# Block-diagonal carried states: one 128-row state product for both heads of a pair

## The chip, the cores and the metric

The kernel runs on one NeuronCore of a Trainium2 chip. The metric is device time in microseconds from start to end of the program; the median of several executions counts. The engines are PE (TensorE, with its weight loads, PEld), DVE (VectorE), ACT (ScalarE), POOL (GpSimd) and SP (SyncE, which issues most DMAs).

## What is computed

Two layers of a hybrid block over 2048 latent and 256 context tokens, 1024 wide. Each layer projects the normed tokens, runs four mixers with four heads of 64 beside each other (differential attention, HGRN2, windowed attention, mLSTM), gates their outputs and projects them back. The change lies in the outputs of two of them. Cut to that, with q, k, v per head and chunk:

```python
# HGRN2: o_t = S_t^T q_t in chunks, forward and backward, then summed
o = (jnp.einsum('bhnls,bhnsv->bhnlv', a, v)                       # within the chunk
     + jnp.einsum('bhnlk,bhnkv->bhnlv', q * jnp.exp(cum), s_start))  # carried state
y = from_heads(rmsnorm(o_f + flip_time(o_b), g))

# mLSTM: each direction has its own denominator
num = (jnp.einsum('bhnls,bhnsv->bhnlv', s, v)
       + g0[..., None] * jnp.einsum('bhnlk,bhnkv->bhnlv', q, c0))  # carried state c0
den = jnp.sum(s, axis=-1) + g0 * jnp.einsum('bhnlk,bhnk->bhnl', q, n0)
hid = num / jnp.maximum(jnp.abs(den), jnp.exp(-m_t))[..., None]
y = rmsnorm(h_f + flip_time(h_b), g) * sigmoid(og)
```

## The kernel before

Tokens are cut into 18 tiles of 128 (16 latent, 2 of context; the second layer needs outputs for 16). Four heads are two pairs (`pr`), and the two heads of a pair (`pa_`) lie in partitions 0 to 63 and 64 to 127 of one tile.

A layer has three stages: the first projections; differential attention, with the other projections as filler between its products; and the final stage. While the last projections run, window attention (`swa_stream`) and mLSTM (`mlstm_stream`) may already do two tiles (`room`, L1227). When the projections are done (`done["rest"]`), their buffers are freed and the output product (`out_stream`) and HGRN (`hgrn_stream`) join. `weave` picks the next step of these streams: each `yield` names a position in tiles, a distance in modelled PE time and a condition, and `mm` (L92) adds to that modelled time by the count of moving columns (four times that for fp32). The order in which each engine gets its instructions comes from a scheduler that works from this written order; each engine then works in order.

`yt_of` hands out one tile of mixed output per token tile, `YTB` of them in all; a stream may begin tile i only while i is less than the number of tiles put out plus `YTB`. HGRN works on groups of two tiles and asks for both.

The carried states at the start of each tile were stored by the projection stage in device memory (`dmC` for mLSTM, 64 x 65 per head, its last column the normalizer; `dhS` for HGRN, 64 x 64). `states_of` (L1232) loads them for two tiles and both directions: one DMA for the forward direction, two for the backward one, whose order is reversed, and a memset where a tile has none before it. The loaded tile has 128 partitions: the two heads of a pair above each other.

In `mlstm_stream`, `mqk` holds the products of keys and queries, DVE multiplies them by the decays in `r1b`, and then for each half `pa_` a PSUM bank `num` takes, for two directions and two pairs, one product of 128 rows (`r1b` by `v1`) and one of the 64 rows of that head (`g0b` by `cst`). ACT takes the absolute denominators, DVE their maximum, reciprocal and the quotient `hd`, and POOL adds the two directions into `yt`. In `hgrn_stream`, for each half a bank `pos` (`go` in the trace) takes for two tiles and two pairs the product within the tile (`Am` by `vi`, 128 rows) and the two directions' state products (`qe` by `hst`, 64 rows), and ACT copies the bank to `O`.

Of the kernel before, what the change touches and what calls it, by code (L numbers as in the profile page):

```python
# [19 lines left out]
YTB, GPB, FXB, EB = 6, 4, 1, 3  # L20
# [13 lines left out]
P = 128  # L34
# [39 lines left out]
def kernel(  # L74
# [29 lines left out]
    def act(o, i, f, **kw):  # L104
        A.activation(out=o, in_=i, func=f, **kw)  # L105
# [153 lines left out]
    for l in range(n_layers):  # L259
# [941 lines left out]
        with ExitStack() as st4:  # L1201
# [30 lines left out]
            def states_of(src, g, n, pool, tag):  # L1232

                st_ = pool.tile([P, 2, 2, 2, n], F32, tag=tag, name=tag, bufs=2)
                for d in range(2):
                    js = [jpos(d, order[2 * g + i]) - 1 for i in range(2)]
                    for i, j in enumerate(js):
                        if j < 0:
                            G.memset(st_[:, d, :, i], 0.0)
                    if min(js) >= 0 and js[0] < js[1]:  # L1240
                        SP.dma_start(st_[:, d], src[d][:, :, js[0]:js[1] + 1])
                    else:
                        for i, j in enumerate(js):
                            if j >= 0:
                                SP.dma_start(st_[:, d, :, i], src[d][:, :, j])
                return st_
# [142 lines left out]
            def mlstm_stream():  # L1389
                nxt = mlstm_load(0)  # L1390
                for i in range(len(order)):
# [3 lines left out]
                    if i % 2 == 0:  # L1395
                        cst = states_of(dmC, i // 2, 65, ml, "cst")
# [10 lines left out]
                    for pa_ in range(2):  # L1407
                        r_ = slice(pa_ * 64, pa_ * 64 + 64)
                        num = bank([P, 4, 65], "mnum")
                        dn = ml.tile([P, 4], F32, tag="dn", name="dn", bufs=4)  # L1410
                        for d in range(2):
                            for pr in range(2):
                                h = pr * 2 + pa_
                                mm(num[:, d * 2 + pr], r1b[:, d, h], v1[:, h], True, False)
                                mm(num[:, d * 2 + pr], g0b[r_, d, pr], cst[r_, d, pr, i % 2], False, True)
                        act(dn, num[:, :, 64], AF.Abs)
                        tt(V, dn.rearrange("p (d a) -> p d a", a=2), dn.rearrange("p (d a) -> p d a", a=2),
                           view(TM, (4 * NT + js[0]) * 4 + pa_, (4 * (NT + js[1] - js[0]), 2), (2, 2)), ALU.max)
                        V.reciprocal(dn, dn)
                        hd = ml.tile([P, 4, 64], F32, tag="hd", name="hd", bufs=1)  # L1420
                        tt(V, hd, num[:, :, 0:64], bc(dn, 2, 64), ALU.mult)
                        tt(G, hq.rearrange("p (a i) d -> p a i d", i=2)[:, :, pa_], hd[:, 0:2], hd[:, 2:4], ALU.add)
                        yield i + 0.5 + 0.4 * pa_, MLW, None
# [12 lines left out]
            def hgrn_stream():  # L1436
# [8 lines left out]
                V.tensor_copy(hgm, hgl_)  # L1445
                for g in range(ngrp):
# [17 lines left out]
                    hst = states_of(dhS, g, 64, hg, "hst")  # L1464
# [65 lines left out]
                    ov = O.rearrange("p (i a c) d -> p i a c d", i=2, c=2)  # L1530
                    for pa_ in range(2):
                        r_ = slice(pa_ * 64, pa_ * 64 + 64)
                        pos = bank([P, 2, 2, 64], "go")
                        for i in range(2):
                            for pr in range(2):
                                o = pr * 256 + i * P
                                h = pr * 2 + pa_
                                po = pos[:, i, pr]
                                mm(po, Am[pa_][:, i, pr], vi[:, i, h * 64:(h + 1) * 64], True, False)
# [187 lines left out]
```

## Time and profile before

| | us |
|---|---|
| median of 3 runs | 4207.11 |
| lowest, highest | 4199.64, 4225.74 |
| the profiled execution | 4225.03 |
| its span, first to last instruction | 4223.2 |

The profile shows the profiled execution alone. Its page lists busy time by engine, the chain that ended last and the costliest groups; the trace behind it can be asked for stretches of time (busy time by engine, granted TensorE clock), for one tile's instructions, for waits and for instructions in order. A matrix product appears as a MATMUL on PE and a LDWEIGHTS on PEld; `mnum<-cst,g0b 64*128 64x65` is a product into `mnum` with 64 rows, 128 weight columns and 65 moving columns. The ends of PE's instructions are modelled, so the price of one is read from start to start. The granted clock is 1 at 2.4 GHz and 0.5 at 1.2 GHz, as a mean over the stretch.

### The profile page before, as it was taken

The numbers are of one execution on the slowest core, as the hardware profiler recorded it, in microseconds if no ns is written. First come the engines' busy times: TensorE is split into PE (matmuls) and PEld (weight loads), VectorE is DVE, ScalarE is ACT, GpSimd is POOL, SyncE is SP. The second block draws the span as 40 slices with busy tenths as digits, with TensorE's granted clock in tenths as the row PEclk, the third lists the DMA queues.
The fourth block names the chain that finished last, engine by engine and source line by source line (L and its number), as shares of the span: only waits on it lengthen the run. The fifth ranks groups of instructions, "written<-read, shape, count | busy, mean of one in ns | idle before, by whom it ended". The sixth has DMA issues, their size and how long they took to land. (4 is left out here: it accounts for less than half of the span.)

```text
span 4223.2 us, 78658 instructions
## 1 busy us (share of the span) xinstructions
PE 3576.0 (85%) x30342; PEld 2404.5 (57%) x30342; DVE 2834.6 (67%) x4343; ACT 2333.8 (55%) x4679; POOL 2355.6 (56%) x1727
## 2 busy tenths in 40 slices
PE   6988878888769986999989887787877798789998
PEld 3656645444547675666657475544454565556665
DVE  5167888889894546556543599888898665555654
ACT  4245656666655545566643366566666565545553
POOL 4443555443445457788757446645334554777763
PEclk9999989999989986889899999999998899678879
DMA  5356856667656546578644467577775662655762
GB/s 204 99 139 151 192 127 164 134 149 157 128 141 163 136 137 145 153 191 190 175 145 139 119 138 153 128 151 154 151 158 126 164 150 92 171 130 147 174 148 78
DMA packets 1256959, 622.19 MB, mean 147 GB/s; under 512 B 913476, under 2 KB 1203848, under 8 KB 1256584
## 3 DMA queue, kind: packets, MB, share of 16 engines
q1 hardware_dynamic: 1154216, 490.64, 51.4%
q10 hardware_dynamic: 102368, 126.52, 9.0%
q8 instruction: 239, 3.92, 0.4%
q14 instruction: 136, 1.11, 0.1%
HBM read 291.76 MB, written 131.23 MB: 100 GB/s over the span
## 5 line engine op out<-in xcount | busy, mean ns | idle before, releaser
L108 POOL TENSOR_TENSOR p<-p,p 128x1024 f16<-128x1024 f32 (+2 forms) x264 | 627.3, 2377 | 786.4 <-ACT p L1084 706.4
L94 PE MATMUL ptm<-wb,hh 128*128 128x256 f16 (+2 forms) x5024 | 839.4, 274 | 31.1 <-DVE dSs L111 8.1
L105 ACT ACTIVATE p<-scr,sm 128x1024 f32<-128x1024 f32 (+2 forms) x528 | 628.0, 1193 | 422.7 <-DVE sm L1073 143.8
L1048 DVE TENSOR_REDUCE sm<-scr 128x1 f32<-128x1024 f32 (+2 forms) x528 | 698.9, 1326 | 214.8 <-PE scr L94 210.9
L94 PE MATMUL pfm<-hh,wb 128*128 128x512 f16 (+1 forms) x2592 | 803.4, 374 | 29.8 <-DVE gz L111 10.2
L94 PE MATMUL ptm<-wb,hl 128*128 128x256 f16 (+2 forms) x2512 | 674.1, 274 | 2.1 <-POOL hl L108 2.1
L94 PEld LDWEIGHTS <-wb 128*128 128x128 f16 x3888 | 376.2, 100 | 407.2 <-issue 72.6
L94 PE MATMUL scr<-Ks,Qs 128*128 128x512 f16 (+1 forms) x1296 | 362.3, 379 | 282.1 <-ACT p L105 279.4
L94 PEld LDWEIGHTS <-hh 128*128 128x128 f16 x5024 | 481.5, 100 | 134.7 <-issue 37.8
L94 PE MATMUL pfm<-hl,wb 128*128 128x512 f16 (+1 forms) x1296 | 484.4, 374 | 0.0
L111 DVE SCALAR_TENSOR_TENSOR p<-p,sm,p 128x1024 f32<-128x1024 f32 (+2 forms) x264 | 414.3, 1570 | 8.1
L94 PE MATMUL fx<-wo,mh 128*128 128x512 f16 x1088 | 370.0, 424 | 7.9 <-DVE yt L108 4.8
L94 PEld LDWEIGHTS <-Qs 128*128 128x128 f16 x1296 | 130.5, 102 | 422.7 <-issue 352.2
L1084 ACT CAST p<-p 128x1024 f16<-128x1024 f32 (+2 forms) x264 | 297.5, 1127 | 40.6 <-DVE p L111 35.4
L94 PEld LDWEIGHTS <-wt 128*128 128x128 f16 x4640 | 239.6, 101 | 80.0 <-DMA wt<-p 27.5
L94 PE MATMUL pv<-Vs,wt 128*128 128x128 f16 (+1 forms) x4640 | 254.1, 212 | 30.4 <-DMA wt<-p 16.4
L94 PEld LDWEIGHTS <-hl 128*128 128x128 f16 x2512 | 251.7, 100 | 35.9 <-POOL hl L108 3.5
L108 POOL TENSOR_TENSOR E<-lk,cm 128x512 f32<-128x512 f32 (+1 forms) x136 | 203.0, 1493 | 49.8 <-PE gA L94 24.7
L94 PE MATMUL fx<-wo,mlo 128*128 128x512 f16 x544 | 228.7, 420 | 1.5 <-DVE mlo L108 1.3
L108 POOL TENSOR_TENSOR ph<-swp,ph 128x640 f16<-128x640 f32 (+2 forms) x136 | 190.2, 1399 | 49.5 <-ACT ph L1326 36.6
L108 DVE TENSOR_TENSOR QQ<-hq,E 128x512 f32<-128x512 f32 x119 | 152.3, 1289 | 90.6 <-ACT E L105 38.2
L105 ACT ACTIVATE E<-E 128x1024 f32<-128x1024 f32 x136 | 143.1, 1052 | 82.7 <-POOL E L108 73.6
(298 smaller groups left out, 6835.2 us busy)
## 6 DMA issues: line engine op xcount, KB each, us to landing
wraw<-in_w_in_dram SPq DMA_DIRECT2D x60, 512.0 KB
dgt<-ga ACTq DMA_DIRECT2D x68, 256.0 KB
r1b<-dr SPq DMA_DIRECT2D x68, 256.0 KB
gtt<-dgt SPq DMA_DIRECT2D x34, 512.0 KB
mraw<-in_w_mod_dram SPq DMA_DIRECT2D x64, 256.0 KB
vi<-dhi SPq DMA_DIRECT2D x49, 256.0 KB
KSb<-dsk SPq DMA_DIRECT2D x56, 192.0 KB
Ks<-dka SPq DMA_DIRECT2D x64, 144.0 KB
```

The costliest lines, as they stand in the source:

```text
L94: PE.matmul(o, lhsT=lhsT, rhs=rhs, start=start, stop=stop)
L105: A.activation(out=o, in_=i, func=f, **kw)
L108: return e.tensor_tensor(out=o, in0=a, in1=b, op=op)
L111: V.scalar_tensor_tensor(out=o, in0=a, scalar=s, in1=b, op0=op0, op1=op1)
L1048: V.tensor_reduce(sm[:, m * 2 + j:m * 2 + j + 1], ps[:, :n], AX.X, ALU.min)
L1084: A.copy(wl[:, :n], p[:, :n])
```

## The change

The two heads' states of a pair are laid block-diagonally: `st_[0:64, ..., 0:n]` holds the first head, `st_[64:128, ..., n:2n]` the second, and the rest is zero, set once in two fixed buffers per mixer (`state_places`) that take turns. So one product of 128 rows gives both heads' state parts side by side, 130 or 128 moving columns wide. Each piece is loaded by a DMA of its own for each half. mLSTM loads its states for each tile instead of for each two. Its banks are cut by direction instead of by half: both directions still have their denominators, but the first direction's quotient is written straight to `yt`, the second's to `hd`, and one addition follows. HGRN has one bank for both halves and one copy out of it. `YTB` goes from 6 to 5.

```diff
-YTB, GPB, FXB, EB = 6, 4, 1, 3
+YTB, GPB, FXB, EB = 5, 4, 1, 3
...
-            def states_of(src, g, n, pool, tag):
-
-                st_ = pool.tile([P, 2, 2, 2, n], F32, tag=tag, name=tag, bufs=2)
+            def states_of(src, ts, n, places, turn):
+
+
+                st_ = places[turn % 2]
                 for d in range(2):
-                    js = [jpos(d, order[2 * g + i]) - 1 for i in range(2)]
+                    js = [jpos(d, t) - 1 for t in ts]
                     for i, j in enumerate(js):
                         if j < 0:
                             G.memset(st_[:, d, :, i], 0.0)
-                    if min(js) >= 0 and js[0] < js[1]:
-                        SP.dma_start(st_[:, d], src[d][:, :, js[0]:js[1] + 1])
-                    else:
-                        for i, j in enumerate(js):
-                            if j >= 0:
-                                SP.dma_start(st_[:, d, :, i], src[d][:, :, j])
+                    for hf in range(2):
+                        r_, c_ = slice(hf * 64, hf * 64 + 64), slice(hf * n, hf * n + n)
+                        if min(js) >= 0 and js[0] <= js[-1]:
+                            SP.dma_start(st_[r_, d, :, :, c_], src[d][r_, :, js[0]:js[-1] + 1])
+                        else:
+                            for i, j in enumerate(js):
+                                if j >= 0:
+                                    SP.dma_start(st_[r_, d, :, i, c_], src[d][r_, :, j])
+                return st_
+
+            def state_places(pool, n, tiles, tag):
+                st_ = [pool.tile([P, 2, 2, tiles, 2 * n], F32, tag=f"{tag}{i}", name=f"{tag}{i}", bufs=1) for i in range(2)]
+                for a in st_:
+                    G.memset(a, 0.0)
                 return st_
...
             def mlstm_stream():
+                places = state_places(ml, 65, 1, "cst")
...
-                    if i % 2 == 0:
-                        cst = states_of(dmC, i // 2, 65, ml, "cst")
+                    cst = states_of(dmC, [order[i]], 65, places, i)
...
-                    for pa_ in range(2):
-                        r_ = slice(pa_ * 64, pa_ * 64 + 64)
-                        num = bank([P, 4, 65], "mnum")
+                    for d in range(2):
+                        num = bank([P, 2, 2, 65], "mnum")
                         dn = ml.tile([P, 4], F32, tag="dn", name="dn", bufs=4)
-                        for d in range(2):
-                            for pr in range(2):
+                        for pr in range(2):
+                            mm(num[:, pr].rearrange("p i c -> p (i c)"), g0b[:, d, pr], cst[:, d, pr, 0], True, False)
+                            for pa_ in range(2):
                                 h = pr * 2 + pa_
-                                mm(num[:, d * 2 + pr], r1b[:, d, h], v1[:, h], True, False)
-                                mm(num[:, d * 2 + pr], g0b[r_, d, pr], cst[r_, d, pr, i % 2], False, True)
-                        act(dn, num[:, :, 64], AF.Abs)
-                        tt(V, dn.rearrange("p (d a) -> p d a", a=2), dn.rearrange("p (d a) -> p d a", a=2),
-                           view(TM, (4 * NT + js[0]) * 4 + pa_, (4 * (NT + js[1] - js[0]), 2), (2, 2)), ALU.max)
+                                mm(num[:, pr, pa_], r1b[:, d, h], v1[:, h], False, pa_ == 1)
+                        nv = num.rearrange("p a i c -> p (a i) c")
+                        act(dn, nv[:, :, 64], AF.Abs)
+                        tt(V, dn, dn, TM[:, 2, d, js[d] * 4:js[d] * 4 + 4], ALU.max)
                         V.reciprocal(dn, dn)
-                        hd = ml.tile([P, 4, 64], F32, tag="hd", name="hd", bufs=1)
-                        tt(V, hd, num[:, :, 0:64], bc(dn, 2, 64), ALU.mult)
-                        tt(G, hq.rearrange("p (a i) d -> p a i d", i=2)[:, :, pa_], hd[:, 0:2], hd[:, 2:4], ALU.add)
-                        yield i + 0.5 + 0.4 * pa_, MLW, None
+                        hd = ml.tile([P, 4, 64], F32, tag="hd", name="hd", bufs=1) if d else hq
+                        tt(V, hd, nv[:, :, 0:64], bc(dn, 2, 64), ALU.mult)
+                        yield i + 0.5 + 0.4 * d, MLW, None
+                    tt(G, hq, hq, hd, ALU.add)
...
+                places = state_places(hg, 64, 2, "hst")
...
-                    hst = states_of(dhS, g, 64, hg, "hst")
+                    hst = states_of(dhS, order[2 * g:2 * g + 2], 64, places, g)
...
-                    ov = O.rearrange("p (i a c) d -> p i a c d", i=2, c=2)
-                    for pa_ in range(2):
-                        r_ = slice(pa_ * 64, pa_ * 64 + 64)
-                        pos = bank([P, 2, 2, 64], "go")
-                        for i in range(2):
-                            for pr in range(2):
-                                o = pr * 256 + i * P
+                    pos = bank([P, 2, 2, 2, 64], "go")
+                    for i in range(2):
+                        for pr in range(2):
+                            o = pr * 256 + i * P
+                            for d in range(2):
+                                mm(pos[:, i, pr].rearrange("p a c -> p (a c)"), qe[:, d, o:o + P], hst[:, d, pr, i], d == 0,
+                                   False)
+                            for pa_ in range(2):
                                 h = pr * 2 + pa_
-                                po = pos[:, i, pr]
-                                mm(po, Am[pa_][:, i, pr], vi[:, i, h * 64:(h + 1) * 64], True, False)
-                                mm(po, qe[r_, 0, o:o + P], hst[r_, 0, pr, i], False, False)
-                                mm(po, qe[r_, 1, o:o + P], hst[r_, 1, pr, i], False, True)
-                        A.copy(ov[:, :, :, pa_], pos)
+                                mm(pos[:, i, pr, pa_], Am[pa_][:, i, pr], vi[:, i, h * 64:(h + 1) * 64], False, pa_ == 1)
                         yield 2 * g + 1.9, 0.0, None
+                    A.copy(O, pos.rearrange("p i a c d -> p (i a c) d"))
```

## Rows read from the trace of the kernel before

**Rows 1.** The page: busy time by engine, and the chain that ended last by line.

```profile
PE 3576.0 (85%) x30342; PEld 2404.5 (57%) x30342; DVE 2834.6 (67%) x4343; ACT 2333.8 (55%) x4679; POOL 2355.6 (56%) x1727
PE fx L94 3%; PE go L94 2%; POOL E L108 1%; POOL yt L108 1%; PE mnum L94 1%; PE ptm L94 0%; DVE QQ L108 0%; DMA swt<-ph 0%; PE gA L94 0%; PE ss L94 0%; PE spv L94 0%; DMA og<-dog 0%; DVE xt L111 0%; POOL ph L108 0%; POOL r1b L108 0%
```

**Rows 2.** Windows, final stages: length; busy PE, PEld, DVE, ACT, POOL; clock; DMA.

```profile
1552.00:2230.00 678.00, 608.04 (x5449) 408.10 (x5449) 372.39 (x641) 389.11 (x1033) 511.29 (x430) 0.82 0.66 171
...
3640.00:4223.00 583.00, 524.69 (x4610) 349.19 (x4608) 324.63 (x534) 307.79 (x848) 406.43 (x337) 0.80 0.57 142
```

**Rows 3.** Windows of layer 0's final stage, same columns: opening, middle, 200 us.

```profile
1600.00:1650.00 50.00, 34.91 (x238) 29.30 (x239) 28.81 (x43) 27.89 (x76) 22.76 (x20) 0.52 0.69 163
1700.00:2150.00 450.00, 431.96 (x4034) 282.72 (x4034) 259.18 (x446) 274.74 (x753) 371.41 (x312) 0.88 0.69 172
...
1800.00:2000.00 200.00, 193.18 (x1822) 129.38 (x1823) 120.69 (x212) 131.35 (x362) 174.29 (x147) 0.89 0.78 186
```

**Rows 4.** Waits of PE, 1700 to 2150 us: releaser, sum in us, times, longest.

```profile
PE spv L94 <- DMA swt<-ph: 6.8, 3, 3.3
...
PE mnum L94 <- DVE r1b L108: 1.7, 1, 1.7
```

**Rows 5.** Windows, `mnum` alone: both final stages; sum with 1290:1552 and 3340:3640.

```profile
1552.00:2230.00 678.00, 104.39 (x495) 84.31 (x494) 13.08 (x31) 5.20 (x31) 0.82 0.66 171
...
3640.00:4223.00 583.00, 75.88 (x400) 62.97 (x400) 10.58 (x25) 4.25 (x25) 0.80 0.57 142
sum 1823.00, PE 220.77 PEld 179.79 DVE 28.73 ACT 11.34; mean PE 55.19 PEld 44.95 DVE 7.18 ACT 2.84
```

**Rows 6.** The same windows, `go` alone: the sum (all in the final stages).

```profile
sum 1823.00, PE 176.15 PEld 151.88 ACT 12.54; mean PE 44.04 PEld 37.97 ACT 3.14
```

**Rows 7.** Timeline of PE (start, duration, product, count): a `mnum` bank's first, and the next.

```profile
3822.37 0.33 PE L94 MATMUL mnum<-v,r1b 128*128 128x65 f32 x2
...
3825.18 0.45 PE L94 MATMUL gA<-QQ,E 64*64 64x64 f32 x14
```

**Rows 8.** Timeline of PE, `go` at both clock levels.

```profile
1690.41 0.43 PE L94 MATMUL go<-vi,Am 128*128 128x64 f32 x2
1690.78 0.66 PE L94 MATMUL go<-hst,qe 64*128 64x64 f32 x4
1691.36 0.43 PE L94 MATMUL go<-vi,Am 128*128 128x64 f32 x2
...
1747.29 1.11 PE L94 MATMUL go<-hst,qe 64*128 64x64 f32 x4
```

**Rows 9.** Timeline of PE, fp32 of 128 rows followed by 128 rows.

```profile
2058.35 0.60 PE L101 MATMUL ft<-ident,yt 128*128 128x128 f32 x4
2058.79 0.22 PE L94 MATMUL ss<-swm 128*128 128x128 bf16 x1
...
2081.29 0.33 PE L94 MATMUL mnum<-v,r1b 128*128 128x65 f32 x2
2081.46 0.38 PE L94 MATMUL ss<-KSc,QS 128*128 128x256 f16 x2
```

**Rows 10.** Groups by form, 1700 to 2150 us: count, busy us, mean ns, idle before.

```profile
L108 DVE TENSOR_TENSOR r1b<-mqk,r1b 128x512 f32<-128x512 f32 x26 | 17.1, 683 | 24.2 <-PE mqk L94 24.2
...
L108 POOL TENSOR_TENSOR yt<-O,ghg 128x256 f32<-128x256 f32 x14 | 11.2, 821 | 3.5 <-DVE O L108 2.8 <-DVE dn L1419 0.7
```

**Rows 11.** Loads of `cst` (ns min/median/max), one of them in the timeline, and its bank.

```profile
L1245 SPq DMA_DIRECT2D cst<-dmC x34: 518/610/1731, 1315.5 to 4035.2; - x34
...
3958.12 1.20 SPq L1245 DMA_DIRECT2D cst<-dmC  x2
...
3967.23 0.33 PE L94 MATMUL mnum<-v,r1b 128*128 128x65 f32 x2
```

**Rows 12.** Tile 10's output on ACT's queue; the last tile's first `mnum` bank (chain).

```profile
4113.27 0.34 ACTq L1615 DMA_DIRECT2D out_dram<-xt  x1
...
4149.02 2.72 PE mnum L94 x16
```

## The prediction

> **What bounds the kernel now.** I read the page's busy shares and its chain first [rows 1]: PE is busy 85% of the span, DVE, POOL and ACT 55 to 67%, and the two products that the change rebuilds, `go` and `mnum`, carry 2% and 1% of the chain that ended last. Next comes the split by stage. The edited code runs in the two final stages [rows 2], where mLSTM, HGRN, window attention and the output product are woven (1552 to 2230 and 3640 to 4223 us), and a little in the ends of the projections before them, where the first mLSTM tiles are woven in. The final stages are 678 and 583 us long; PE is busy 608.0 and 524.7 of them, 0.90 in both, and POOL comes next with 511.3 and 406.4. A closer look at layer 0's [rows 3] shows a middle where PE works 432.0 of 450 us, 96%. The opening is different: from 1600 to 1650 PE works 34.9 of 50 us at a granted clock of 0.52, near the lower of its two levels. The list of who waited for whom confirms the middle [rows 4]: PE's largest wait in 450 us sums to 6.8. So PE has hardly anything there that it waits for today, and a microsecond taken off its products is one off the stage, until another engine sets the pace. Whether POOL does so is the open question.
>
> How much of PE this is: `mnum` takes 220.8 us over the four stretches, 104.4 + 75.9 = 180.3 of it in the final stages [rows 5]; `go` takes 176.2, all in the final stages [rows 6].
>
> **The products.** Each fp32 product of the program is two matrix instructions in the trace. In the old `mnum` bank, a pair over 128 rows alternates with a pair over 64 rows; the bank's 8 products take 2.81 us from 3822.37 to the next instruction at 3825.18 [rows 7], 0.35 each. Two banks are 5.62 us per tile at the full clock (recorded over 34 tiles: 6.5, since part runs at the lower level). The old `go` repeats one pair over 128 rows and two over 64: 0.95 us from 1690.41 to 1691.36 [rows 8], eight times per group of two tiles, 7.6 us (recorded over 17 groups: 10.4).
>
> What a pair costs when the row count does not change is seen in three places. A `mnum` pair over 128 rows that happens to be followed by another 128-row product is done in 0.17 us, 0.085 an instruction; four fp32 transposes with 128 rows, 128 weight columns and 128 moving columns take 0.44, 0.11 each [rows 9]; four 64-row instructions of `go` behind each other take 0.58, 0.145 each [rows 8]. The new products all have 128 rows and 128 weight columns, with 130, 128, 65 or 64 moving columns: nearest to the transposes. I take 0.11 and keep 0.085 and 0.145 as ends. Per tile, `mnum` goes from 16 products to 12 (4 for the states of both heads, 8 within the chunk), 24 instructions, 2.64 us against 5.62: 53% less (ends 38 and 64%). Per group, `go` goes from 24 products to 16, 32 instructions, 3.52 against 7.6: 54% less (ends 39 and 64%). On the recorded sums that is 117 + 95 = 212 us of PE (ends 152 and 254); 180.3 x 0.53 + 176.2 x 0.54 = 191 of it lie in the final stages and 21 in the ends of the projections.
>
> **From PE to the span.** In the final stages PE's 1133 us become 942, and POOL has 918. POOL's own change is small: two additions into `yt` become one over the same elements, at most the 0.82 us of a 128x256 one [rows 10] per tile, taken as 0. The new zeroing of the buffers is two memsets of 128x1024 and two of 128x520 per layer; no row has one of that size, and by that addition they are at most 4 x 0.82 and 2 x 0.82 each, 10 us a layer, and nothing if other work covers them; I take 5. With PE and POOL level at some 930 us in 1261, I do not expect either to reach 0.90. POOL's best 200 us today are 174.3, or 0.87, beside a PE at 0.97 [rows 3]; over a whole stage with its opening I take 0.83 for PE: 942 / 0.83 = 1135 us for 1261, 126 us gained of the 191. The ends are 942 / 0.90 = 1047 (all of it) and hardly any gain if POOL already sets the pace. Of the 21 us in the ends of the projections I count half, 10, as the projections' own products lie behind them.
>
> PE's other row speaks for the low end: weight loads fill 408.1 of 678 us, less than POOL's 511.3 [rows 2]. The Trainium skill, "Perfetto Trace Analysis", section Identifying the Most-Contended Engine, holds that the busy time of matmuls is no good measure for TensorE, since they are pipelined, and that the share of weight loads should be read instead. By it POOL is the most contended engine of the stage, and the sum would gain some 40 us, as the first rival has it, not 126. The timeline's start-to-start times, which do not rest on modelled ends, show no holes in the middle, so I keep PE as the bound.
>
> **What costs.** (a) Loads: the state of one tile now comes in four DMAs, where two tiles took three, and HGRN's in six per group, where it was three: four more per tile, 0.61 us each on SP [rows 11], 2.4 us of a tile's 36 (583 / 16). A `cst` load issued from 3958.1 to 3959.3 serves a bank that starts at 3967.2 [rows 11], 8 us of lead that hide it: 0. At most it is 2.4 x 30 = 73 if that lead is gone, since `r1b`, `g0b` and the transposed weights of window attention queue behind it on SP, and `mnum` and `spv` wait for those. (b) The bank of one direction needs all four heads, so its products within the chunk wait for both DVE products on `mqk`, 0.68 us each [rows 10], where the first bank needed one. PE waited 1.7 us for these in 450 us [rows 4]; at most 0.68 x 34 = 23, I take 5. (c) ACT copies `go` in one instruction instead of two: the same elements, off PE's path, 0; all copies together are 12.5 us [rows 6], so at most that either way. (d) Five `yt` buffers instead of six. In the opening, tile 5 may not start before tile 0 is out: its products leave the opening, where PE waits anyway. Its `mnum` alone is 6.5 us of PE; with the rest of the tile's mLSTM and window attention I allow 15. It is lost only as far as nothing else fills the hole: 5 us a layer, ends 0 and 15. Later, tile 15 takes the buffer of tile 10 instead of tile 9. Tile 10's output goes out at 4113.3, and the first bank of `mnum` for tile 15 starts at 4149.0 [rows 12], 36 us behind it: one output tile of slack, so 0.
>
> The paces that weave the streams stay as they are: `mm` counts a product by its moving columns, and 16 x 65 equals 4 x 130 + 8 x 65, as 24 x 64 equals 8 x 128 + 8 x 64. The written order moves only with (d).
>
> Sum: 126 + 10 gained; 5 for (b), 2 x 5 for (d) and 2 x 5 for the memsets lost; 136 - 25 = 111, say 110 us. The profiled execution took 4225 us (span 4223.2), 0.4% above the median of the runs, 4207; 4225 - 110 = 4115, and on the median's scale 4097. I forecast **4095 us**.
>
> **Rivals.** First, POOL is the bound already: it keeps its 918 us and its waits, and only what `go` and `mnum` hold of the chain, 2% + 1% of 4223, 127 us [rows 1], is cut by a third, some 40: 4225 - 40, or 4167 on the median's scale. For it: POOL's 0.87 in the busiest 200 us [rows 3]. Against it: PE's few waits [rows 4]. Chance 0.17.
>
> Second, the clock. Four equal instructions of `go` take 0.66 us at 1690 and 1.11 at 1747 [rows 8]: within the same kind of run the granted clock is at the upper or the lower level. If more idle time on PE brought the final stages from 0.81 to 0.75, 12% more of 1135 us would run at the lower level, 136 us at 1.7 times the price: 56 lost, 4150. Chance 0.10.
>
> Third, everything arrives, because shorter fp32 runs leave PE as dense as before: 212 - 25 gained, 4038, or 4020 on the median's scale. Chance 0.10.
>
> Fourth, on the other side: the ring of five. A group of HGRN asks for two tiles at once, so it may start when tile 2g - 4 is out, where 2g - 5 was enough, one output tile or 36 us earlier. If each of 17 groups lost 10 us by it, 170 us would stand against the 120 that are left without (d): slower, some 4260. It decides from 7 us per group on. For it: HGRN's chain of `E`, `QQ` and `gA` is the longest per tile, and POOL's `E` is in the chain [rows 1]. Against it: the 36 us of slack [rows 12]. Chance 0.13.
>
> **How the numbers follow.** The forecast has 0.50, with a range of its own of 4045 to 4155. A change of 1% (42 us) is about what a measurement of this kernel can tell from none. Faster by more than that: the forecast, the third rival, most of the clock's case and a little under half of the first: 0.72. Within 1%: 0.17. Slower: 0.11. The range runs from the third rival's time to above the first's and leaves out the tail beyond the third and most of the fourth: 4020 to 4205.
>
> **What would show it.** Right: `go` at about 3.5 us a group and `mnum` at 2.6 a tile at the full clock, evenly spaced; PE in the middles of the final stages at 80 to 90% and POOL above 85%; final stages near 615 and 525 us. Wrong: new products at 0.15 us or more an instruction (then 60 us of PE's gain go); PE waiting for `cst` or `hst` loads; holes on POOL in front of `E` that end with an output tile (the ring); a granted clock below 0.78 in the final stages.

## The result and the profile after

The changed kernel takes 4095.72 us, the median of four runs (4092.26 to 4102.18); the kernel before takes 4203.38, the median of its three runs and a fourth (4192.92 to 4225.74). The ratio is 0.974, with an interval of 0.970 to 0.978: 108 us faster. The forecast was 4095, and the range held the time. The profiled execution took 4102.18 us, with a span of 4100.4, so between the two profiles 123 us are to be found.

From the page of the kernel after: busy time by engine, and the chain that ended last, by line (they answer to [rows 1]).

```profile
PE 3358.2 (82%) x29798; PEld 2269.8 (55%) x29798; DVE 2831.4 (69%) x4343; ACT 2330.9 (57%) x4662; POOL 2375.0 (58%) x1701
...
POOL E L108 2%; PE fx L94 1%; POOL yt L108 1%; POOL ph L108 1%; DMA cm<-dhc 1%; PE ptm L94 0%; DMA g0b<-dg 0%; POOL r1b L108 0%; SPq L1385 0%; DMA swt<-ph 0%; PE go L94 0%; DMA gtt<-dgt 0%; POOL g0b L108 0%; SPq L1383 0%; PE gA L94 0%
```

PE lost 218 us of busy time; DVE, ACT and POOL kept theirs within 20. `go` fell from 2% of the chain to under 1, and `mnum` is no longer among its largest parts.

To see where the 123 us went, both traces are cut into four stretches at the same events: the last of HGRN's states written and the last tokens of layer 0 written. First the kernel before, by windows: stretch, length, busy PE, PEld, DVE, ACT and POOL, granted clock, DMA share, GB/s.

```profile
0.00:1553.00 1553.00, 1284.05 (x10602) 861.87 (x10602) 1084.63 (x1653) 827.94 (x1452) 711.98 (x487) 0.94 0.60 147
1553.00:2215.00 662.00, 596.92 (x5384) 398.47 (x5383) 361.71 (x625) 381.45 (x1018) 499.69 (x417) 0.82 0.66 169
2215.00:3629.00 1414.00, 1159.57 (x9642) 785.51 (x9642) 1055.13 (x1518) 808.89 (x1339) 727.20 (x477) 0.94 0.60 140
3629.00:4223.20 594.20, 535.46 (x4716) 358.66 (x4716) 333.18 (x549) 315.56 (x870) 416.69 (x348) 0.80 0.57 142
```

The kernel after, same view and columns; the last two lines are the middles of its final stages.

```profile
0.00:1549.00 1549.00, 1277.15 (x10584) 860.14 (x10585) 1083.25 (x1652) 828.22 (x1452) 716.32 (x490) 0.93 0.60 147
1549.00:2169.00 620.00, 507.54 (x5113) 350.86 (x5111) 357.35 (x626) 379.10 (x1010) 508.52 (x400) 0.83 0.71 176
2169.00:3582.00 1413.00, 1154.60 (x9627) 779.29 (x9626) 1056.37 (x1519) 808.60 (x1339) 730.62 (x478) 0.93 0.61 142
3582.00:4100.40 518.40, 418.88 (x4480) 279.52 (x4479) 334.48 (x548) 315.02 (x862) 419.55 (x335) 0.89 0.66 164
...
1700.00:2100.00 400.00, 342.45 (x3542) 239.05 (x3539) 231.25 (x421) 261.23 (x715) 350.63 (x282) 0.87 0.74 186
3700.00:4030.00 330.00, 286.08 (x3163) 189.00 (x3162) 227.23 (x383) 218.96 (x627) 295.60 (x242) 0.95 0.72 178
```

The stretches differ by 4, 42, 1 and 76 us: the gain lies in the two final stages, and almost nothing is left in the projections. Together the final stages take 1138 us instead of 1256, with 926 us of PE instead of 1132. PE went from 0.90 of them to 0.82 and 0.81. In the middles POOL is busy 0.88 and 0.90, PE 0.86 and 0.87: the two are level, where in layer 0's middle before PE alone stood at 0.96 [rows 3].

The rebuilt products and the output product `fx`, each alone, summed over 1250 to 2260 and 3200 to 4230 us of the kernel after (for the first two see [rows 5, 6]); in this order `mnum`, `go`, `fx`.

```profile
sum 2040.00, PE 120.45 PEld 112.84 DVE 28.58 ACT 11.17; mean PE 60.22 PEld 56.42 DVE 14.29 ACT 5.59
...
sum 2040.00, PE 84.11 PEld 77.97 ACT 9.73; mean PE 42.06 PEld 38.98 ACT 4.87
...
sum 2040.00, PE 413.86 DVE 46.46; mean PE 206.93 DVE 23.23
```

`mnum` lost 100 us and `go` 92. `fx`, which the change doesn't touch, lost 44: in the kernel before the same view gives it this.

```profile
sum 2040.00, PE 458.02 DVE 46.45; mean PE 229.01 DVE 23.23
```

The timeline of PE in the kernel after (start, duration, product, count): a whole `mnum` bank up to the next product, and a quarter of a `go` group up to the next (they answer to [rows 7, 8]).

```profile
3717.51 0.39 PE L94 MATMUL mnum<-cst,g0b 128*128 128x130 f32 x2
3717.74 0.56 PE L94 MATMUL mnum<-v,r1b 128*128 128x65 f32 x4
3718.13 0.44 PE L94 MATMUL mnum<-cst,g0b 128*128 128x130 f32 x2
3718.41 0.56 PE L94 MATMUL mnum<-v,r1b 128*128 128x65 f32 x4
3718.80 0.59 PE L94 MATMUL fx<-wo,mh 128*128 128x512 f16 x2
...
3751.88 0.61 PE L94 MATMUL go<-hst,qe 128*128 128x128 f32 x4
3752.33 0.56 PE L94 MATMUL go<-vi,Am 128*128 128x64 f32 x4
3752.72 0.59 PE L94 MATMUL fx<-wo,mh 128*128 128x512 f16 x2
```

The `mnum` bank's 12 instructions take 1.29 us, 0.108 each, where the old bank took 2.81 [rows 7]; the quarter of `go` takes 0.84 us for 8, 0.105 each, where three products of the old `go`, six instructions, took 0.95 [rows 8]. Most single records of these two lines of work start 0.11 us apart, whether they have 130, 128, 65 or 64 moving columns.

### The profile page after: what moved, and what is told of

Same layout as the page of the kernel before. It is cut to its first block, busy times and chain, and to the rows that moved or that the text cites. A ratio compares the mean times of both kernels' runs of the same rounds, so it can differ in the third digit from the quotient of the medians.

```text
span 4100.4 us, 77666 instructions
## 1 busy us (share of the span) xinstructions
PE 3358.2 (82%) x29798; PEld 2269.8 (55%) x29798; DVE 2831.4 (69%) x4343; ACT 2330.9 (57%) x4662; POOL 2375.0 (58%) x1701
## 5 line engine op out<-in xcount | busy, mean ns | idle before, releaser
L94 PE MATMUL fx<-wo,mh 128*128 128x512 f16 x1088 | 342.4, 396 | 16.8 <-DVE xt L111 8.5
L94 PE MATMUL fx<-wo,mlo 128*128 128x512 f16 x544 | 212.9, 391 | 1.4 <-DVE mlo L108 1.1
L108 DVE TENSOR_TENSOR QQ<-hq,E 128x512 f32<-128x512 f32 x119 | 143.8, 1214 | 65.2 <-ACT E L105 46.7
```

The source lines that it names most:

```text
L94: PE.matmul(o, lhsT=lhsT, rhs=rhs, start=start, stop=stop)
L108: return e.tensor_tensor(out=o, in0=a, in1=b, op=op)
```

## Experiments

Each ratio is to runs of the kernel before on the same chip. The theory is that of the prediction: PE sets the pace of the final stages, and what is dear in the old banks is the change of the row count from product to product. The rivals are that POOL paces, that the clock does, and that the shorter list of products, not their rows, brings the gain.

### Rows or number: the products of 128 rows, but one for each head

```diff
-mm(num[:, pr].rearrange("p i c -> p (i c)"), g0b[:, d, pr], cst[:, d, pr, 0], True, False)
...
-    mm(num[:, pr, pa_], r1b[:, d, h], v1[:, h], False, pa_ == 1)
+    mm(num[:, pr, pa_], r1b[:, d, h], v1[:, h], True, False)
+    mm(num[:, pr, pa_], g0b[:, d, pr], cst[:, d, pr, 0, pa_ * 65:pa_ * 65 + 65], False, True)
```

(and `go` in the same way, against the kernel after.)

> The changed kernel, but each head has a state product of its own again: 128 rows (the zero half counted in), 65 or 64 moving columns. As many products as before the change (16 for a tile of mLSTM, 24 for a group of HGRN), all of 128 rows. Theory (the change of row count is dear, a product itself is cheap): an instruction costs 0.11 us as in the changed kernel, a mnum bank 1.7 us where it was 2.81 and is 1.29; PE's sum for mnum and go about 285 us (397 before, 204 after); some 4140 us. Rival (the count of products is what costs): a bank stays at 2.8 us, the sum near 397, 4200 us.

Measured: 4123.29 us, ratio 0.982 (0.978 to 0.985), 81 us faster than before. Its bank has as many products as the old one, in the timeline of PE:

```profile
3747.30 0.33 PE L94 MATMUL mnum<-v,r1b 128*128 128x65 f32 x2
3747.47 0.39 PE L94 MATMUL mnum<-cst,g0b 128*128 128x65 f32 x2
...
3749.03 0.59 PE L94 MATMUL fx<-wo,mh 128*128 128x512 f16 x2
```

1.73 us for 16 instructions, 0.108 each, against 2.81 with 64 and 128 rows in turn [rows 7]. So as many instructions cost 1.08 us less a bank when the rows don't change, 0.13 us for each of its eight changes of rows. The old `go` gives about the same price: its six instructions take 0.95 us, 0.30 above six of 0.108, with two changes, 0.15 each [rows 8]. The Trainium skill, "TensorEngine Tiling (Array Packing)", Key Properties, says that changing the tiling mode drains the TensorE; a price at each change of rows fits that, though no row here shows whether it is a drain. The rival, a bank of 2.8 us and 4200 in all, is refuted. `mnum` takes 70 us less than before and `go` 52 (150.5 and 123.8 us); as the run keeps the rest of the change too (banks by direction, loads, five buffers), the 81 us are not the rows' alone. The smaller number seems to bring the rest: in medians 27 us more, but the two intervals just touch.

### Each mixer alone

`e_mlonly` keeps mLSTM's half of the change and puts HGRN's and the six buffers back; `e_hgonly` keeps HGRN's half and the five buffers.

```diff
-YTB, GPB, FXB, EB = 5, 4, 1, 3
+YTB, GPB, FXB, EB = 6, 4, 1, 3
...
-                    hst = states_of(dhS, order[2 * g:2 * g + 2], 64, places, g)
+                    hst = states_old(dhS, g, 64, hg, "hst")
...
+                                mm(po, Am[pa_][:, i, pr], vi[:, i, h * 64:(h + 1) * 64], True, False)
+                                mm(po, qe[r_, 0, o:o + P], hst[r_, 0, pr, i], False, False)
+                                mm(po, qe[r_, 1, o:o + P], hst[r_, 1, pr, i], False, True)
```

> mLSTM as changed, HGRN as before, six yt buffers. Theory (PE's time is passed on to the span at a fixed rate): half of PE's gain, 100 of 192 us, and no cost for the ring: some 4147 us. Rival (POOL cuts the gain off): this half alone already brings 80 us or more, below 4125, and the two halves add up to more than both together.

> HGRN as changed, mLSTM as before, five yt buffers. Theory (PE's time is passed on at a fixed rate): 92 of 192 us of PE's gain, some 4155 us. Rival (POOL cuts the gain off): this half alone brings 70 us or more, below 4133.

Measured: `e_mlonly` 4153.68, ratio 0.988 (0.985 to 0.991), 51 us; `e_hgonly` 4124.60, ratio 0.980 (0.976 to 0.984), 80 us. The final stages of `e_mlonly`, by windows:

```profile
1548.00:2192.00 644.00, 552.50 (x5259) 373.89 (x5258) 361.87 (x627) 379.38 (x1018) 503.83 (x401) 0.83 0.68 174
3590.00:4158.00 568.00, 493.11 (x4612) 333.82 (x4612) 327.05 (x550) 313.26 (x870) 412.03 (x334) 0.81 0.59 150
```

and of `e_hgonly`:

```profile
1555.00:2175.00 620.00, 544.84 (x5237) 368.54 (x5236) 364.30 (x624) 377.49 (x1009) 506.22 (x417) 0.86 0.68 176
3583.00:4125.60 542.60, 468.08 (x4584) 309.72 (x4584) 344.40 (x549) 313.32 (x862) 424.31 (x348) 0.86 0.62 157
```

Each half makes its own product cheap (`mnum` 116.5 us in the first, `go` 84.6 in the second). The halves sum to 131 us, the whole is 108, but the intervals (some 22 and 18 us either way) leave open whether the second half really brings less. Neither expectation holds for both: `e_mlonly` lies near the theory's time, `e_hgonly` below the 4133 of its rival. What is clear is that the larger of the two removals, 104 us of `mnum`, brings less than the 92 us of `go`. With HGRN changed the granted clock is 0.86 in both stages, where it was 0.82 and 0.80, `fx` falls from 458.0 to 430.6, and PE loses 119 us in the two final stages. With mLSTM changed the clock is 0.83 and 0.81, `fx` falls to 446.6 only, the old `go` beside it rises from 176.2 to 191.2, and PE loses 87. The clocks of whole executions say the same: 0.913 to 0.921 in the four runs of `e_hgonly` and 0.904 to 0.910 in those of `e_mlonly`, where the 40 runs of the kernel before that stand beside the experiments have 0.901 to 0.911.

### The old `go`, cut into pieces

The kernel before, with a step between its groups of three products, so that other streams' products come between:

```diff
+                                if (i, pr) != (1, 1):
+                                    yield 2 * g + 1.85, HGW, None
```

> The kernel before, with places between the groups of three products of go (one over 128 rows, two over 64) where other streams' products may come in; the products are the same. Theory (the granted clock falls because go is one long run of slow fp32 products, and what follows it pays): the clock in the middles of the final stages rises from 0.83 to 0.88 towards 0.9, fx gets cheaper by 15 us or more, and the time falls by 10 to 30 us. Rival (the clock follows PE's total load, or go's runs have no part in it): clock and time as before, 4195 to 4215.

Measured: 4181.10 us, ratio 0.995 (0.993 to 0.997): 20 us faster, with the same products. `fx` alone in this kernel, the same sum as above, and the middles of the final stages by windows; the last two lines are the same middles in the kernel before:

```profile
sum 2040.00, PE 433.66 DVE 46.41; mean PE 216.83 DVE 23.21
...
1700.00:2100.00 400.00, 386.01 (x3747) 258.72 (x3746) 231.79 (x403) 256.18 (x716) 341.99 (x285) 0.91 0.70 181
3700.00:4030.00 330.00, 301.14 (x2978) 201.48 (x2976) 192.04 (x325) 189.19 (x523) 258.66 (x219) 0.87 0.62 156
...
1700.00:2100.00 400.00, 382.90 (x3574) 250.17 (x3573) 226.69 (x389) 245.73 (x674) 329.50 (x278) 0.88 0.71 177
3700.00:4030.00 330.00, 305.81 (x2779) 203.27 (x2778) 182.99 (x315) 184.66 (x508) 247.05 (x209) 0.83 0.61 150
```

Without a single product less, `fx` falls by 24 us and `go` by 19 (176.2 to 156.7), while `mnum` rises by 7. That is more than two kernels differ whose time is that of the kernel before: `e_yt5` and `e_before_lo` below have 456.2 and 451.7 us of `fx`. Fewer of `fx`'s products ran at the lower clock (the last section has the count). The clock of these middles goes from 0.88 to 0.91 and from 0.83 to 0.87, but that the clock as a whole rose is not shown: `e_yt5` has 0.89 and 0.85 there, and over whole executions the mean is 0.907 in ten runs with `go` cut up and 0.906 in 19 of the kernel before. So without the long rows of changing products `fx` and `go` cost less; whether the rows held the clock down, or the new order only moved the slow time to other products, this run leaves open.

### Less dense work: one of the three output products left out

In the kernel before and in the kernel after, the product of the low part of the mixed output with the weights is left out, and its modelled time is counted as before, so that the streams are woven alike.

```diff
-                            mm(ps, mh[:, k], wo[1][:, k, s_], False, False)
-                            mm(ps, ml_[:, k], wo[0][:, k, s_], False, k == KC - 1)
+                            mm(ps, mh[:, k], wo[1][:, k, s_], False, k == KC - 1)
+                            pe_ns[0] += 512 / 2.4
```

> The kernel before without the third product of the output (low half of the activations by the weights), its place in the modelled pace kept: 544 instructions and 229 us of PE less, all in the final stages. Theory (PE paces the final stages before the change, other engines' chains come up behind it): as much off PE as the change took, with what the clock gave, so as much off the time, 90 to 120 us: 4085 to 4115. Rival (PE's share was not the point; the change gained by something else): less than 50 us.

> The changed kernel without the third product of the output, 213 us of PE less. Theory (PE paces the changed kernel's final stages only in part; the last 70 us that merging took off PE gave 27): 0.2 to 0.4 us a microsecond, 4010 to 4055. Rival one (PE still paces it alone): 100 us or more, below 3996. Rival two (PE has nothing left to give): 15 us or less, above 4080.

Measured: the kernel before without it 4171.86 us, ratio 0.993 (0.990 to 0.995), only 27 us faster; the kernel after without it 4062.76, ratio 0.968 (0.964 to 0.972), 33 us faster than after, by intervals that overlap a little. The first is a miss: 90 to 120 us were expected, and less than 50 was the mark of the rival, that PE's share was not the point. The second lies between its theory (to 4055) and its second rival (from 4080). The final stages of the first, by windows:

```profile
1554.00:2211.00 657.00, 564.58 (x5097) 394.91 (x5096) 360.31 (x626) 381.48 (x1018) 504.25 (x417) 0.76 0.67 170
3624.00:4171.00 547.00, 479.64 (x4460) 342.28 (x4460) 335.97 (x550) 316.03 (x870) 419.91 (x348) 0.77 0.61 156
```

and of the second:

```profile
1544.00:2141.00 597.00, 455.45 (x4812) 324.29 (x4811) 372.11 (x619) 376.64 (x1006) 506.04 (x401) 0.79 0.72 181
3554.00:4061.70 507.70, 385.06 (x4220) 278.50 (x4219) 336.98 (x548) 314.59 (x862) 420.29 (x334) 0.80 0.69 167
```

In the kernel before `fx` falls by 139 us (to 318.9); the page's two groups of `fx` sum to 599 us where its window has 458, since overlapping products count once there, so 229 for the left-out group was too much to expect. PE's busy time falls by 88 alone (1132 to 1044): the clock fell from 0.82 and 0.80 to 0.76 and 0.77, and products that were left became dearer, `ss` from 130.1 to 141.9 and `mnum` from 220.8 to 225.9 (`go` fell from 176.2 to 164.0). In the kernel after it is 123 of `fx` and 86 of PE, with the clock down from 0.83 and 0.89 to 0.79 and 0.80. Taking these dense fp16 products away lowered the clock (over whole executions 0.881 to 0.892 in five runs, where the kernel before beside them has 0.903 to 0.909), as taking HGRN's slow fp32 ones away raised it. That the two kernels gain about alike for 88 and 86 us of PE, where PE had been 0.90 and 0.82 busy, speaks against a sharp point at which PE stops to count; that the first gains only 0.31 us for a us of PE remains a point for its rival.

### POOL: moved, and taken away

A flag of the written order moves the subtraction that makes `ph`'s low part from POOL to DVE, in the kernel after and in the kernel before.

```diff
-    [38826.0, 42669.0, 12000.0, 977.0, 2924.0, 1746.0, 500.0, 500.0, 2.6, 600.0, 0.22, 1, 1, 0],
-    [40000.0, 23476.0, 6974.0, 719.0, 313.0, 1000.0, 500.0, 500.0, 2.658, 0.0, 0.22, 1, 0, 0],
+    [38826.0, 42669.0, 12000.0, 977.0, 2924.0, 1746.0, 500.0, 500.0, 2.6, 600.0, 0.22, 0, 1, 0],
+    [40000.0, 23476.0, 6974.0, 719.0, 313.0, 1000.0, 500.0, 500.0, 2.658, 0.0, 0.22, 0, 0, 0],
```

> The changed kernel with one operation moved: the subtraction that makes the low halves of window attention's weights (ph, 1.44 us, 136 of them, 196 us in all) runs on DVE instead of POOL. Theory (after the change POOL and PE set the pace of the final stages together): POOL gets 150 us less there, and the time falls by 15 to 50 us, to 4045 to 4080. Rival (PE alone still sets the pace): no more than 10 us either way, 4085 to 4105; if DVE's own queue suffers, slower than 4105.

> The same move in the kernel before the change. Theory (before the change PE set the pace of the final stages, POOL did not): within 15 us of the kernel before, 4190 to 4220, so that the move is worth more after the change than before it. Rival (POOL set the pace already): it falls as much as in the changed kernel, 20 us or more.

Measured: after 4112.50, ratio 0.980 (0.976 to 0.983), 17 us slower than the kernel after, by intervals that overlap a little, as the expectation had it for the case that DVE's own queue suffers; before 4197.40, ratio 1.000 (0.998 to 1.001), no difference. POOL got rid of 117 us in the final stages of the first (928 to 811), and nothing was gained: the gain expected of a POOL that paces beside PE is refuted in this form. PE's largest waits in the kernel after, and then in the one with the subtraction on DVE, both from 1700 to 2100 us (releaser, sum in us, times, longest):

```profile
PE spv L94 <- DMA swt<-ph: 21.0, 11, 3.7
PE gA L94 <- DVE QQ L108: 17.5, 11, 4.5
PE ft L101 <- DVE hd L108: 4.7, 3, 2.4
```

```profile
PE spv L94 <- DMA swt<-ph: 11.1, 7, 3.7
PE ft L101 <- DVE hd L108: 10.6, 6, 5.1
PE gA L94 <- DVE hd L108: 4.6, 2, 2.6
```

In this window PE waits less for `ph` and more for `hd`, but its wait for `QQ` is gone, so that all waits for DVE together do not grow (30 and 26 us). Over both final stages they do, from 91 to 104 us, while those for `swt<-ph` fall from 60 to 49: what PE gained on one engine it lost on the other. That the some 50 instructions a stage that went to DVE stand ahead of what PE needs from it is the likely reason; no run takes it apart.

So in the next one POOL's work is taken away, not moved. The kernel after leaves out the gate, the multiplication of `yt` by `gtt`:

```diff
-                    tt(G, yt[:, 0:512], yt[:, 0:512], gt_[:, 0:512], ALU.mult)
-                    tt(G, yt[:, 512:], yt[:, 512:], gt_[:, 512:], ALU.mult)
```

> The changed kernel without the multiplication of the mixed output by its gate: 68 POOL operations of 1.27 us, 86 us of POOL less, and one step less ahead of the output's transposes. Theory (POOL is one of several that pace the changed kernel): 15 to 40 us less, 4055 to 4080. Rival (moving work off POOL is worth nothing, as with ph): 10 us or less.

Measured: 4049.64 us, ratio 0.964 (0.961 to 0.967), 46 us faster than the kernel after. Its final stages by windows:

```profile
1549.00:2124.00 575.00, 486.22 (x5114) 329.67 (x5114) 363.68 (x627) 376.84 (x1009) 460.98 (x365) 0.88 0.75 190
3530.00:4047.20 517.20, 423.59 (x4478) 286.65 (x4477) 339.46 (x548) 312.96 (x862) 374.67 (x302) 0.88 0.66 164
```

POOL has 836 us in place of 928, the stages are 46 us shorter, nearly all of it in layer 0, and PE's own 926 became 910, with the clock of layer 0's stage at 0.88 instead of 0.83. The gain is past the 15 to 40 us expected. PE's waits for `swt<-ph`, the transfer of what POOL makes, fall from 60 to 43 us in the two stages, so POOL's work counts in the kernel after. How much is not shown: the gate also stands between the mixers and the transposes that `fx` waits for, so part of the gain is a shorter chain, and part comes with the 16 us of PE, which this run doesn't separate.

### The ring of `yt` buffers

The kernel before with five buffers:

```diff
-YTB, GPB, FXB, EB = 6, 4, 1, 3
+YTB, GPB, FXB, EB = 5, 4, 1, 3
```

> The kernel before with five yt buffers instead of six, nothing else. Theory: the opening of each final stage loses one tile of cover, 5 us a layer: some 4213 us against 4203. Rival (the ring of five holds HGRN up in each group): 50 us or more, 4255 us and above.

Measured: 4196.21 us, ratio 0.999 (0.997 to 1.002): the sixth buffer is worth nothing there. The reverse, six buffers in the kernel after, needs room, so its output weights are loaded in pieces of 64 columns; `e_after_braw` has the pieces alone.

```diff
-YTB, GPB, FXB, EB = 5, 4, 1, 3
+YTB, GPB, FXB, EB = 6, 4, 1, 3
...
-                    raw = fo.tile([P, KC, P], F32, tag="braw", name="braw", bufs=1)
+                    for s_ in (slice(b * P, b * P + 64), slice(b * P + 64, b * P + P)):
+                        raw = fo.tile([P, KC, 64], F32, tag="braw", name="braw", bufs=1)
```

> The changed kernel with six yt buffers again; the room comes from loading the output weights in pieces of 64 columns instead of 128. Theory (with PE's load lower, a fifth buffer more or less matters as little as before the change): within 12 us of the changed kernel, 4084 to 4108. Rival (the ring of five costs in the faster kernel, where streams run closer behind the output): 20 us or more faster, below 4076.

> The changed kernel with the output weights loaded in pieces of 64 columns and five yt buffers: the control for the run with six. Theory (the smaller pieces cost what that run lost, the sixth buffer nothing): 4108 to 4125. Rival (six buffers cost): 4085 to 4103, as the changed kernel.

Measured: six buffers with pieces 4118.42, ratio 0.981 (0.977 to 0.985); the pieces alone 4079.00, ratio 0.971 (0.968 to 0.974). With the pieces held equal, the sixth buffer costs 39 us, by intervals that don't overlap. The first run's expectation had that on neither side; it is the rival of the second, though the time lies 6 us below that rival's range. The final stages are 632 and 530 us long with six buffers and 605 and 522 with five, PE's busy time 947 and 920 us. Why more room slows the kernel stays open: a longer lead changes the written order of all streams, and no run here takes that apart. The pieces alone are the fastest complete kernel of the study, but their interval overlaps that of the kernel after, so they are not shown to be faster.

## Why the prediction was right, and where its steps were off

**PE as the bound: right in direction, too strict in form.** Eight of the kernels, ordered by PE's busy time in the two final stages together; the last column is the time gained, in medians, against the kernel before on the same chip:

| kernel | PE busy, us | POOL busy, us | length, us | gained, us |
|---|---|---|---|---|
| before | 1132 | 916 | 1256 | 0 |
| split `go` | 1095 | 920 | 1219 | 20 |
| mLSTM alone | 1046 | 916 | 1212 | 51 |
| before, two output products | 1044 | 924 | 1204 | 27 |
| HGRN alone | 1013 | 931 | 1163 | 80 |
| not merged | 971 | 920 | 1163 | 81 |
| after | 926 | 928 | 1138 | 108 |
| after, two output products | 841 | 926 | 1105 | 136 |

POOL's work is within 15 us of the same in all of them, and the length falls by 151: POOL does not set the pace alone. The length follows PE, by 118 us for 206 from before to after, 0.57, and by 34 for 86 below that, 0.39. As the profile of before is a long execution, the medians give less: 0.31 to 0.67 us for a us of PE in the single kernels, 108 for 206 or 0.52 in the whole change. (From the profile of `e_yt5`, an execution near the median with 1121 us of PE in 1255, it is 116 for 195, 0.60.) The prediction passed on 126 of 191, 0.66. The step that was too strong is its sentence that a microsecond off PE is one off the stage until another engine takes over; there is no such corner. As PE is relieved, its waits come back one by one. In the final stage of layer 0, the largest waits of PE in the kernel before, and then after (same view as above, 1553 to 2215 and 1549 to 2169 us):

```profile
PE spv L94 <- DMA swt<-ph: 16.2, 5, 6.3
PE gA L94 <- DVE QQ L108: 15.7, 8, 5.9
PE ss L94 <- ACT swp L105: 7.2, 4, 3.5
```

```profile
PE gA L94 <- DVE QQ L108: 31.0, 15, 7.8
PE spv L94 <- DMA swt<-ph: 29.9, 16, 3.7
PE ss L94 <- ACT swp L105: 17.6, 9, 2.6
```

The three sums double, from 39 to 79 us. PE's busy time fell by 89 us in this stage and its length by 42; these waits hold 39 of the 47 between.

**The price of an instruction: right.** 0.11 us was taken and 0.105 to 0.108 measured. The 0.145 kept as an end, read off four 64-row instructions of `go` as a case without a change of rows, holds one: in the trace's single records the two neighbours in their midst start 0.11 us apart too, and the rest is the changes before and behind. A group of `go` costs 3.4 us (32 x 0.105; forecast 3.52), a tile's `mnum` 2.58 (2.64). In recorded time `go` lost 92 us (95), `mnum` 100 (117). The miss on `mnum` is in the scaling: a ratio of start-to-start times was applied to recorded time, and recorded time over start-to-start was 6.5 / 5.62 = 1.16 before and is (120.45 / 34) / 2.58 = 1.37 now. Part of this is the modelled ends: the records of the new bank end at 3718.97, 0.17 us behind the start of the next product, those of the old one (3824.81 + 0.43) 0.06 behind [rows 7], which for 68 banks is some 7 of the 17 us. A larger share at the lower clock it is not: by the start-to-start times of neighbouring records 0.15 of `mnum`'s are slow in both kernels. The rest stays open.

**The clock: missing from the sum, and of the other sign.** 926 us of PE in the final stages were nearly foretold (942), but by errors that cancel: there the two products gave 178 us, not 191 (`mnum` 184.2 to 98.0, `go` 176.2 to 84.1), `fx` gave 44 that no term had, and PE as a whole lost 16 less than these sum to. The second rival let the clock fall by more idle time on PE; it rose, to 0.83 and 0.89, and over whole executions to 0.913 to 0.922. The cut-up `go` shows that `fx` can be made cheaper without removing a product, and the left-out `fx` products show the fall that the rival feared, with PE at 0.86 and 0.88 busy, more than in the kernel after. It is PE's busy time as recorded, clock included, that the length follows. A stretch's mean clock also counts the time in which PE is idle and so is not what the products pay: in layer 0 it stands at 0.82 before and 0.83 after, yet `fx` fell there from 241.5 to 215.3 us.

**The costs: too high.** 25 us were set against the gain. (d) was put at 10 and measured as nothing in the kernel before. (b), the wait of the direction's bank for both DVE products, was put at 5: PE's idle time in front of `mnum` that ended with `r1b` went from 14.3 to 7.1 us over the program. (a) is right: in the tile view of `cst`, PE waited 1.3 us in all for one load. The zeroing of the buffers in the kernel after (ns min/median/max, first and last start):

```profile
L1254 POOL MEMSET cst<- x4: 532/532/533, 1285.2 to 3289.4; 128x520 f32 x4
...
L1254 POOL MEMSET hst<- x4: 951/952/952, 1541.5 to 3566.1; 128x1024 f32 x4
```

Two of 0.53 and two of 0.95 us are 3 us of POOL a layer, where 5 were taken. Of these costs no more than some 7 us can be found, 3 for each layer's zeroing and 1.3 for the load. The profiled executions differ by 123 us, 118 from the final stages and 5 from the projections; with the 7 that is 130 of gain, where 126 + 10 stood, less 7 of cost, where 25 stood. So the gain was 6 too high, the costs 18 too high, and by its own scale the sum was 12 us short (111 for 123). The medians differ by 108 (4203 to 4096), because the profile of before is one of its longer executions, so part of how close 4095 came is luck.

**By layer.** 615 and 525 us were foretold for stretches of 678 and 583, 63 and 58 less. Measured is 42 less and 76 less: the second layer got more than its share, and there the clock rose most, from 0.80 to 0.89 (0.83 to 0.95 in its middle, where layer 0's has 0.88 before and 0.87 after). Why it rose less in layer 0 no run tells.

**The rivals.** POOL as the bound already, 4167: refuted by the table, and with it the reading by weight loads. By the rule of the Trainium skill, "Perfetto Trace Analysis", Identifying the Most-Contended Engine, which reads TensorE by weight loads and MFU (not worked out here), POOL with 916 us was ahead of the weight loads' 757 and some 40 us were to be gained; measured are 108, so the trace does not bear that out here. Near the end of the gain the rival has a point: in the kernel after, POOL's work counts too (the gate left out). The ring of five, 4260: refuted by the two runs with the number of buffers changed, one without effect and one against it. Everything arrives, 4020: no. Of what was to be seen, the evenly spaced products, 80 to 90% for PE and over 85% for POOL in the middles, and the absence of waits for `cst` (but for those 1.3 us) and `hst`, all came.

## What to carry to other kernels

Products with few rows (64 here) that lie between products with all 128 cost more than their columns tell: fill them up to 128 rows with zeros, block-diagonally if two can share one, and price them by start-to-start times of neighbours with the same row count. On an engine that is 90% busy, count on about half of what is taken off it (0.31 to 0.67 here), not all, and look for the engine that is level with it afterwards. Judge a change to PE by the recorded time of the products it leaves alone too: they show what it does to the work beside it.

## What the hardware showed beyond that

- An fp32 pair costs the same with 65 and 130 moving columns (0.108 us an instruction in both), so the zeros of the block-diagonal states are free in time. The Trainium skill, "TensorE: Matmul & The Clock Gate", LDWEIGHTS (loading the stationary operand), puts the time of a weight load on its number of columns, not of rows; the trace agrees: in the kernel before, the median fp32 load of 128 columns for `go` takes 188 ns with 64 rows and 190 with 128.
- The granted clock did not go with PE's busy share in these kernels. In the kernel before PE was busy 0.90 of the final stages at 0.82 and 0.80; after, at 0.82 and 0.81 busy, it was granted 0.83 and 0.89. With HGRN's half alone it was 0.86 in both; leaving out a third of the dense `fx` products lowered it by 0.06 and 0.03 over the stages, at 0.86 and 0.88 busy.
- The clock can be read from one form of product. Of the kernel after, the tile view of `fx` gives (ns min/median/max):

```profile
L94 PE MATMUL fx<-wo,mh x1088: 376/379/634, 1643.1 to 4092.2; 128*128 128x512 f16 x182
```

  The kernel before has the same 376, 379 and 634 for the same 1088 products; what differs is the mean in the page's groups (count, busy us, mean ns, idle before), here of the kernel before:

```profile
L94 PE MATMUL fx<-wo,mh 128*128 128x512 f16 x1088 | 370.0, 424 | 7.9 <-DVE yt L108 4.8
```

  and of the kernel after:

```profile
L94 PE MATMUL fx<-wo,mh 128*128 128x512 f16 x1088 | 342.4, 396 | 16.8 <-DVE xt L111 8.5
```

  If the products took either 379 or 634 ns, 18% of them were slow before, (424 - 379) / 255, and 7% after. With `go` cut up the mean is 407, 11%; with a third of `fx` left out of the kernel before 438, 23%. Why the clock falls where it does, no run here tells.
